# Attention block: the bias and the sums of weights in other slots

## The chip, the cores and the metric

One core of a Trainium2 chip runs the whole kernel. The metric is device time in microseconds, the median of several executions.

## The reference

One pre-norm layer of attention over 4096 tokens of width 1024, with 16 query heads and 4 key heads of 64, a causal window of 128, a learned bias per distance bucket and head, a sink per head, a SiLU gate, the residual, and a final norm:

```python
xn = rms_norm(x, norm_g)
q, k, v, z = split(xn @ w_in)                      # 1024, 256, 256, 1024 columns
s = q @ k.T / 8 + t5_table[bucket(distance)]       # distance 0 to 127 only
p = softmax([s, sink])[..., :-1]
y = ((p @ v) * silu(z)) @ w_out
out = rms_norm(x + y, final_g)
```

## The kernel before, in words

The tokens are cut into 16 blocks of 256. Each block has its projections q, k, v and z, four softmax pairs (a pair is 128 tokens and two key heads; each has two halves with steps scores, post, exps, normalise, turn, and then values and gate), and the output projection o. Every product in 16 bits is made of three passes over a high and a low half; the halves come from a split: ScalarE (ACT) writes the high half, VectorE (DVE) the low half.

A large product of two by two blocks can be done plainly with 8 block products, or as a chain of 7 with sums of blocks as factors (s1 to s4 on the weights, t1 to t4 on x for q and z; for o the sums s are of y and t of the weights). The first blocks run plainly, `PLAIN = {"q": 2, "z": 3, "o": 3}`, since the sums of weights must first be made. `sums` does that for four quarters c of each weight: it loads 1 MB of raw weights `wst`, scales it by the norm's gain (ACT), forms four sums on GpSimd (POOL, in place) and splits each. The q sums go to resident tiles `wq`, those of z and o to DRAM (`wzs`, `wos`; names such as `wzss1` are the tile of sum s1), from which four rotating buffers `ws` stream them. `wst` here has the tag of `xin`, the tile into which the next block's x rows are loaded for the norm, so both take turns in one buffer. `xf` is x transposed, `xb` and `xs` are the splits of it and of its sums.

The order of work is written as a table of slots: block tb starts at slot 25 tb, `at(phase, slot, f)` puts a piece of work there, and `emit` walks through slots and phases. Up to slot `STATIC` a scheduler then reorders each engine's instructions; behind it PE, ACT, DVE and POOL keep the written order. SyncE (SP) issues nearly all loads from one queue, ACT's queue issues the writes of split weights to DRAM.

`make_bias` forms a row of 256 biases per head on TensorE, writes 64 copies per head to DRAM (`scr`), and reads them back skewed by one element per copy, so that partition p holds the bias of query p. It is emitted at slot 8. `open_attn` closes the pool `ramp` of the first raw weights and opens the pool of the softmax tiles.

Of the kernel before, what the change touches and what calls it, by code (L numbers as in the profile page):

```python
# [58 lines left out]
def tile_swa_block(ctx, tc, x, xt, t5, norm_g, final_g, w_q, w_kv, w_z, sinks, w_out, hot, out):  # L59
# [68 lines left out]
    wq = [const.tile([P, 4, 2, 512], F16, name=f"wq{n}") for n in range(NRES)]  # L128
    wkv = const.tile([P, KC, 2, 512], F16, name="wkv")
    wqs = {n: dram.tile([P, 4, 2, 512], F16, name=f"wqs{n}") for n in range(NRES, 7)}  # L130
    wzs = {n: dram.tile([P, 4, 2, 512], F16, name=f"wzs{n}") for n in set(LEFT) | set(BLOCKS)}
    wos = {n: dram.tile([P, 4, 2, 512], F16, name=f"wos{n}") for n in set(RIGHT) | set(BLOCKS)}

    def split(hi, lo, f, scale):
        nc.scalar.activation(hi, f, AF.Copy, scale=scale)
        nc.vector.scalar_tensor_tensor(lo, f, scale, hi, op0=OP.mult, op1=OP.subtract)  # L136

    def load_kv(kc):
        st = work.tile([P, 512], F32, tag=("q00", "q01", "q10", "q11", "z00", "z01", "z10", "z11")[kc], name="wst",
                       bufs=1)  # L140
        nc.sync.dma_start(st, w_kv[kc * P:(kc + 1) * P, :])
        return st

# [6 lines left out]
    def factor(name, left, st):  # L150

        def blk(i, j):
            return st[:, j - 1, (i - 1) * 512:i * 512] if left else st[:, i - 1, (j - 1) * 512:j * 512]

        if name[0] not in "st":
            return blk(int(name[0]), int(name[1]))
        dst, l, r, op = {"s1": ((2, 1), (2, 1), (2, 2), OP.add), "s2": ((2, 1), (2, 1), (1, 1), OP.subtract),
                         "s3": ((1, 1), (2, 2), (2, 1), OP.subtract), "s4": ((1, 2), (1, 2), (2, 1), OP.subtract),
                         "t1": ((1, 2), (1, 2), (1, 1), OP.subtract), "t2": ((1, 2), (2, 2), (1, 2), OP.subtract),
                         "t3": ((1, 1), (1, 2), (1, 1), OP.subtract), "t4": ((2, 1), (2, 1), (1, 2), OP.subtract)}[name]  # L160
        nc.gpsimd.tensor_tensor(blk(*dst), blk(*l), blk(*r), op=op)  # L161
        return blk(*dst)
# [26 lines left out]

    def sums(w, c, left, to):  # L190

        st = work.tile([P, 2, D], F32, tag="xin", name="wst", bufs=1)
        load_pair(w, c, st)
        if left:
            for j in range(2):
                nc.scalar.activation(st[:, j, :], st[:, j, :], AF.Copy, scale=gs[:, 4 * j + c:4 * j + c + 1])  # L196
# [4 lines left out]
    def sum_q(n, name, c, f):  # L201
        if n < NRES:
            split(wq[n][:, c, 0], wq[n][:, c, 1], f, 1.0)
        else:
            to_dram(wqs[n], c, f, 1.0)

    def sum_z(n, name, c, f):
        to_dram(wzs[name], c, f, 1.0)

    def sum_o(n, name, c, f):  # L210
        to_dram(wos[name], c, f, SO)


    ji = const.tile([P, P], I32, name="ji")
    nc.gpsimd.iota(ji, pattern=[[1, P]], base=0, channel_multiplier=-1)
# [3 lines left out]
    nc.vector.tensor_scalar(own_m, ji, 0.0, None, op0=OP.is_ge)  # L219
    ij = const.tile([P, HD], I32, name="ij")  # L220
    for a in range(2):
# [3 lines left out]

    pre = const.tile([P, 2, P], F32, name="pre")
    nc.vector.memset(pre[:, 0, HD:], -BIG)
# [83 lines left out]
    def left_q(name):  # L311
        n = LEFT.index(name)
        return (lambda kc, wi: wq[n][:, kc, wi, :]) if n < NRES else stream("q", name)

# [141 lines left out]
    def make_bias():  # L456
        th = const.tile([BUCKETS, H], F32, name="th")
        nc.sync.dma_start(th, t5)
        hb = work.tile([BUCKETS, 2 * WIN], F32, tag="mc", name="hb", bufs=4)
        nc.sync.dma_start(hb, hot)  # L460
        s1 = const.tile([P, H], F32, name="s1")
        nc.sync.dma_start(s1, bass.AP(tensor=sinks.tensor, offset=sinks.offset, ap=[[0, P], [1, H]]))
        pe = ps("tp", 2)
        nc.tensor.matmul(pe[:H, :2 * WIN], th, hb, start=True, stop=True)
# [4 lines left out]
        for e in range(2):  # L469

            src = bass.AP(tensor=scr.tensor, offset=scr.offset + e * HD * 2 * WIN + HD - 1,
                          ap=[[2 * WIN - 1, HD], [2 * HD * 2 * WIN, H // 2], [1, HD + P]])
            nc.sync.dma_start(bias[e * HD:(e + 1) * HD], src)
# [196 lines left out]
    def at(phase, s, f, *a):  # L670
        work_of[s][phase].append(lambda: f(*a))
# [110 lines left out]

    def block(tb):
# [102 lines left out]
    for c in range(4):  # L886
        st = (work.tile([P, 2, D], F32, tag="ws", name="wst", bufs=4) if c < 3 else
              ramp.tile([P, 2, D], F32, tag="raw3", name="wst", bufs=1))
        raw["q", c] = load_pair(w_q, c, st)
    for c in range(3):  # L890
        raw["z", c] = load_pair(w_z, c, ramp.tile([P, 2, D], F32, tag=f"raw{c}", name="wst", bufs=1))
    for i in range(2):
        x_split(0, i)()
        for kc in range(4 * i, 4 * i + 4):
            split(wkv[:, kc, 0], wkv[:, kc, 1], kv[kc], gs[:, kc:kc + 1])
    for name in BLOCKS:
        for c in range(4):
# [12 lines left out]

# [49 lines left out]
```

## Time and profile before

| | |
|---|---|
| median of three runs | 1416.72 us (1415.52 to 1419.03) |
| profiled execution | 1415.16 us, span 1413.4 us |
| busy: PE, DVE, ACT, POOL | 95%, 83%, 62%, 29% |
| mean granted TensorE clock | 0.989 |
| moved by DMA | 371.96 MB, 263 GB/s |

Line numbers (L327) are those of the kernel before. A name like `c<-s,bias` says what an instruction writes and reads. L327 are the products of q and z, L346 and L408 those of k and v, L506 the scores, L562 the transposes of the weights p, L589 the products with v, L631 the products of o, L464 the bias, L531 and L533 the bias add and the row maximum, L161 the sums on POOL, L135 and L136 the two halves of a split, L196 the scaling of raw weights.

### The profile page before, as it was taken

The numbers are of one execution on the slowest core, as the hardware profiler recorded it, in microseconds if no ns is written. First come the engines' busy times: TensorE is split into PE (matmuls) and PEld (weight loads), VectorE is DVE, ScalarE is ACT, GpSimd is POOL, SyncE is SP. The second block draws the span as 40 slices with busy tenths as digits, with TensorE's granted clock in tenths as the row PEclk, the third lists the DMA queues.
The fourth block names the chain that finished last, engine by engine and source line by source line (L and its number), as shares of the span: only waits on it lengthen the run. The fifth ranks groups of instructions, "written<-read, shape, count | busy, mean of one in ns | idle before, by whom it ended". The sixth has DMA issues, their size and how long they took to land.

```text
span 1413.4 us, 39463 instructions
## 1 busy us (share of the span) xinstructions
PE 1348.6 (95%) x16234; PEld 1086.1 (77%) x16234; DVE 1175.1 (83%) x2847; ACT 878.4 (62%) x2313; POOL 416.3 (29%) x402
## 2 busy tenths in 40 slices
PE   5888999898989999999999999999999999999986
PEld 4887668587578787978788797978879687888842
DVE  7579787778769889798988979898888989888884
ACT  7466666666556566566666656666566666666662
POOL 1001342434323233241322324142322424141124
PEclk9999999999999999999999999999999999999999
DMA  9985657878969677684948767594966769384665
GB/s 370 276 303 183 252 193 299 308 256 325 367 237 334 219 281 270 216 340 168 348 180 297 266 236 300 206 343 159 337 240 250 270 227 353 142 318 176 246 231 208
DMA packets 73253, 371.96 MB, mean 263 GB/s; under 512 B 9040, under 2 KB 11120, under 8 KB 41456
## 3 DMA queue, kind: packets, MB, share of 16 engines
q1 hardware_dynamic: 63968, 351.61, 68.3%
q10 hardware_dynamic: 9104, 17.83, 3.3%
q8 instruction: 127, 2.08, 0.6%
q14 instruction: 54, 0.44, 0.1%
HBM read 332.71 MB, written 36.70 MB: 261 GB/s over the span
## 4 chain that ended last, share of the span: by engine, by line
PE 72%; DVE 10%; DMA 8%; ACT 6%; issue 2%; POOL 2%; SPq 0%; POOLq 0%; ACTq 0%; DVEq 0%
PE pb L327 14%; PE pa L327 14%; PE pc L631 9%; PE o L589 5%; PE pa L631 5%; PE pc L327 5%; PE s L506 5%; PE pc L408 4%; PE pb L346 4%; PE tp L562 3%; PE pb L631 3%; DMA wzs<-ws 1%; DVE wsp L136 1%; DMA wst<-in_wz 1%; POOL wst L161 1%
## 5 line engine op out<-in xcount | busy, mean ns | idle before, releaser
L327 PEld LDWEIGHTS <-ws 128*128 128x128 f16 x6864 | 391.8, 98 | 30.3 <-issue 26.7
L631 PEld LDWEIGHTS <-yo 128*128 128x128 f16 x1380 | 134.0, 99 | 159.9 <-issue 9.3
L327 PEld LDWEIGHTS <-wq 128*128 128x128 f16 x4128 | 237.2, 98 | 15.7 <-issue 10.5
L541 ACT ACTIVATE c<-c,m 128x129 f32<-128x129 f32 x512 | 198.5, 391 | 24.6 <-DVE m L533 24.1
L631 PE MATMUL pc<-ws,yo 128*128 128x512 f16 x768 | 178.1, 382 | 5.1 <-DMA ws<-wos 2.4
L533 DVE CUSTOM_DVE_ANT_0 c<-s,bias,sink 128x128 f32<-128x128 f32 x496 | 153.4, 349 | 7.5 <-PE tp L562 0.3
L247 POOL TENSOR_TENSOR rr<-ms,mhalf 128x1 f32<-128x1 f32 x64 | 36.8, 582 | 353.1 <-DVE ms L245 288.7
L569 DVE SCALAR_TENSOR_TENSOR pt<-tp,pt 128x512 f16<-128x512 f32 x128 | 87.5, 685 | 49.1 <-ACT pt L566 48.9
L553 ACT ACTIVATE c<-c,rl 128x128 f32<-128x128 f32 x256 | 86.8, 393 | 62.7 <-DVE rl L546 62.0
L625 DVE TENSOR_TENSOR yo<-y,yo 128x512 f16<-128x512 f32 x103 | 85.1, 827 | 45.6 <-ACT yo L624 45.4
L506 PE MATMUL s<-K,q 128*128 128x192 f16 x1024 | 109.5, 246 | 12.1 <-DVE m L533 6.1
L549 DVE TENSOR_SCALAR c<-c,rl 128x128 f32<-128x128 f32 x256 | 116.5, 497 | 4.0
L356 ACT ACTIVATE mc<-pa 128x512 f32<-128x512 f32 x68 | 40.5, 595 | 120.0 <-PE pa L327 111.7
L327 PE MATMUL pb<-xb,ws 128*128 128x128 f16 x1776 | 108.5, 221 | 6.2 <-issue 3.9
L161 POOL TENSOR_TENSOR wst<-wst 128x512 f32<-128x512 f32 x48 | 69.9, 1467 | 145.1 <-ACT wst L196 84.4
L327 PE MATMUL pb<-xs,ws 128*128 128x128 f16 x1872 | 111.0, 219 | 0.0
L506 PEld LDWEIGHTS <-q 128*128 128x128 f16 x1024 | 85.3, 98 | 27.5 <-issue 8.2
L570 DVE TENSOR_TENSOR pm<-pt,own_m 128x1024 f16<-128x1024 f16 x128 | 97.5, 761 | 3.7
L617 POOL TENSOR_TENSOR y<-y,y 128x512 f32<-128x512 f32 x52 | 78.9, 1518 | 70.2 <-DVE y L596 48.6
L285 POOL TENSOR_TENSOR xf<-xf 128x512 f32<-128x512 f32 x56 | 74.8, 1347 | 83.4 <-DVE xb L274 74.4
L541 ACT ACTIVATION_READ_ACCUMULATOR c<-c,m 128x1 f32 x512 | 96.5, 188 | 0.0
L631 PE MATMUL pa<-ws,yo 128*128 128x512 f16 x384 | 92.7, 393 | 3.8 <-DVE z L449 3.1
(122 smaller groups left out, 2648.2 us busy)
## 6 DMA issues: line engine op xcount, KB each, us to landing
ws<-wos SPq DMA_DIRECT2D x63, 1024.0 KB, 6.4
ws<-wzss SPq DMA_DIRECT2D x52, 1024.0 KB, 6.6
ws<-wost SPq DMA_DIRECT2D x52, 1024.0 KB, 6.0
ws<-wzs SPq DMA_DIRECT2D x47, 1024.0 KB, 6.2
ws<-wqs SPq DMA_DIRECT2D x28, 1024.0 KB, 5.9
xin<-in_x SPq DMA_DIRECT2D x32, 512.0 KB, 4.6
xf<-in_xt SPq DMA_DIRECT2D x32, 512.0 KB, 4.3
r<-in_x SPq DMA_DIRECT2D x32, 512.0 KB, 5.7
```

The costliest lines, as they stand in the source:

```text
L161: nc.gpsimd.tensor_tensor(blk(*dst), blk(*l), blk(*r), op=op)
L327: nc.tensor.matmul(place(p, c), left(kc, wi)[:, c * P:(c + 1) * P], right_x(tb, right, kc, xi), start=fresh and c == 0 and k == 0, stop=c ...
L506: nc.tensor.matmul(s[:, hp, 0:3 * HD], lhs, rhs, start=hl == 0, stop=hl == 1)
L533: nc.vector.tensor_tensor_reduce(out=cu, in0=sv, in1=b, scale=-1.0 / SCORE, scalar=sink[:, g, r, hp:hp + 1], op0=OP.add, op1=OP.min, accum ...
L541: nc.scalar.activation(cu, cu, AF.Exp, bias=self.m[:, u:u + 1], scale=-1.0, accum_out=self.l[:, u:u + 1])
L549: nc.vector.tensor_scalar(cu[u], cu[u], rl[:, u:u + 1], None, op0=OP.mult)
L553: nc.scalar.activation(cu[u], cu[u], AF.Copy, scale=rl[:, u:u + 1])
L569: nc.vector.scalar_tensor_tensor(w[:, 1], p, SP, w[:, 0], op0=OP.mult, op1=OP.subtract)
L570: nc.vector.tensor_tensor(m.rearrange("p l (h q) -> p (l h) q", h=4), w.rearrange("p l (h q) -> p (l h) q", h=4), own_m[:, None, :].to_bro ...
L617: nc.gpsimd.tensor_tensor(Y[(tb, *dst)], Y[(tb, *l)], Y[(tb, *r)], op=op)
L625: return lambda: nc.vector.tensor_tensor(yo[:, 1], s, yo[:, 0], op=OP.subtract)
L631: nc.tensor.matmul(p, YO[left][:, yi, c * P:(c + 1) * P], right(c, wi), start=fresh and k == 0, stop=k == 11, skip_group_check=not fresh)
```

## The change

The bias is made first: its inputs are loaded right behind block 0's x, the copies are 16 per head in place of 64, and the skewed bias is read in 8 pieces of 16 partitions in place of 2 of 64, behind the raw q weights. The pairs of block 0 stand 4, 3, 2 and 1 slots earlier, and the softmax pool opens at slot 12 in place of 18. `sums` is taken apart into steps with slots of their own and takes a buffer of its own, `stage`. The quarters of q, z and o start at slots 15, 39 and 63, six slots apart (before: 38 to 50, 63 to 75, 88 to 100), and `STATIC` falls from 105 to 90. All q sums go through DRAM; s1 and s2 come back into the plain blocks' tiles `wq[1]` and `wq[2]`, and s3 is streamed for blocks 2 to 4 and then kept in `stage`. The sums are formed in an order that overwrites other blocks. In blocks 0 to 2 the splits of the next x stand later (`PLAIN_X`). Of the differences dv one buffer is left in place of two. At the start the splits of w_kv are written ahead of those of x.

```diff
+    load_xin(0)
+    th = const.tile([BUCKETS, H], F32, name="th")
+    nc.sync.dma_start(th, t5)
+    hb = work.tile([BUCKETS, 2 * WIN], F32, tag="mc", name="hb", bufs=4)
+    nc.sync.dma_start(hb, hot)
+    load_xf(0)
+    nc.scalar.dma_start(gs, norm_g.rearrange("(c p) -> p c", p=P))
+    s1 = const.tile([P, H], F32, name="s1")
+    nc.scalar.dma_start(s1, bass.AP(tensor=sinks.tensor, offset=sinks.offset, ap=[[0, P], [1, H]]))
...
-    NRES = 5
-    STATIC = 105
+    STATIC = 90
+    SUMS = {"q": 15, "z": 39, "o": 63}
+    FIFTH = 5
...
-        st = work.tile([P, 2, D], F32, tag="xin", name="wst", bufs=1)
-        load_pair(w, c, st)
+        keep = []
+        def load():
+            keep.append(load_pair(w, c, work.tile([P, 2, D], F32, tag="stage", name="wst", bufs=1)))
+        def scale(j):
+            nc.scalar.activation(keep[0][:, j, :], keep[0][:, j, :], AF.Copy, scale=gs[:, 4 * j + c:4 * j + c + 1])
+        at("load", s, load)
         if left:
             for j in range(2):
-                nc.scalar.activation(st[:, j, :], st[:, j, :], AF.Copy, scale=gs[:, 4 * j + c:4 * j + c + 1])
-        for n, name in enumerate(LEFT if left else RIGHT):
-            if name[0] in "st":
-                to(n, name, c, factor(name, left, st))
+                at("high", s + 3, scale, j)
+        for i, (n, name) in enumerate((n, name) for n, name in enumerate(LEFT if left else RIGHT) if name[0] in "st"):
+            at("sum", s + 4 + i // 2, lambda name=name: keep.append(factor(name, left, keep[0])))
+            at_split(s + 5 + i // 2, lambda n=n, name=name, i=i: to(s + 5 + i // 2, n, name, c, keep[1 + i]))
+    def sum_to(s, where, c, f, scale):
+        w = work.tile([P, 2, 512], F16, tag="wsp", name="wsp", bufs=3)
+        nc.scalar.activation(w[:, 0], f, AF.Copy, scale=scale)
+        at("turn", s + 1, lambda: nc.scalar.dma_start(where[:, c], w))
+        return lambda: nc.vector.scalar_tensor_tensor(w[:, 1], f, scale, w[:, 0], op0=OP.mult, op1=OP.subtract)
...
-        scr = dram.tile([H, HD, 2 * WIN], F32, name="scr")
-        nc.sync.dma_start(scr, row[:, None, :].to_broadcast([H, HD, 2 * WIN]))
+        COPIES = 16
+        scr = dram.tile([H, COPIES, 2 * WIN], F32, name="scr")
+        nc.sync.dma_start(scr, row[:, None, :].to_broadcast([H, COPIES, 2 * WIN]))
...
-                 zplain=(11, 12, 13, 14, 15, 16, 17, 17), xload=8, pairs=moved(STEADY["pairs"], (7, 5, 4, 2)))
+                 zplain=(11, 12, 13, 14, 15, 16, 17, 17), xload=8, pairs=moved(STEADY["pairs"], (3, 2, 2, 1)))
...
+    PLAIN_X = dict(xsplit=(21, 22), xsum={"t1": 22, "t2": 24, "t3": 26, "t4": 27},
+                   xsumsplit={"t1": 23, "t2": 25, "t3": 29, "t4": 28})
...
-            for n in range(NRES, 7):
+            for n in range(4 if tb < FIFTH else 5, 7):
                 at("load", S["q"][n] - 4, load_s, "q", LEFT[n], wqs[n])
...
-    at("load", 8, make_bias)
-    work_of[18]["bank"].insert(0, open_attn)
+    work_of[12]["bank"].insert(0, open_attn)
...
-        at("soft", SLOTS + (13, 17, 21, 25)[c], sums, w_q, c, True, sum_q)
+        sums(SUMS["q"] + 6 * c, w_q, c, True, sum_q)
...
+    for n in (1, 2):
+        at("load", SLOTS * PLAIN["q"] - 6 + n, lambda n=n: nc.sync.dma_start(wq[n], wqs[n]))
+    at("load", SLOTS * FIFTH - 10, load_fifth)
```

What the scheduler made of it, at three places. First SyncE's queue from the start. Before:

```order
L99 DMA xin<-in_x 128x1024 x2
L105 DMA xf<-in_xt 128x1024 x2
L141 DMA wst<-in_wkv 128x512 x8
L147 DMA wst<-in_wq 128x1024 x8
L147 DMA wst<-in_wz 128x1024 x6
L99 DMA xin<-in_x 128x1024 x2
L105 DMA xf<-in_xt 128x1024 x2
L458 DMA th<-in_t_table 32x16
```

And in the change (its line numbers differ: L111 is L141, L156 is L147, L488 the write of the copies, L496 the skewed read):

```order
L99 DMA xin<-in_x 128x1024 x2
L116 DMA th<-in_t_table 32x16
L118 DMA hb<-in_hot 32x256
L105 DMA xf<-in_xt 128x1024 x2
L497 DMA gf<-in_final_g 128x1024
L111 DMA wst<-in_wkv 128x512 x3
L488 DMA scr<-row 256x1x256
L111 DMA wst<-in_wkv 128x512 x5
L156 DMA wst<-in_wq 128x1024 x8
L496 DMA bias<-scr 16x8x192 x8
L156 DMA wst<-in_wz 128x1024 x6
```

The whole bias, with the final gain gf, now stands ahead of the raw z weights, and five of the eight loads of w_kv and all of w_q stand behind the write of the copies.

Second DVE, where block 0's first softmax steps stand. Before, behind the evacuations of z and the first splits of w_out (`wsp<-r`):

```order
L449 SCALAR_TENSOR_TENSOR z<-z,pb 128x512
L136 SCALAR_TENSOR_TENSOR wsp<-r,wsp 128x512 x2
L449 SCALAR_TENSOR_TENSOR z<-z,pc 128x512
...
L274 TENSOR_TENSOR xb<-xf,xb 128x4x256
L524 COPY_PREDICATED s<-sel,s 128x2x64 x2
L531 TENSOR_TENSOR c<-s,bias 128x128 x4
```

In the change, ahead of the first of them (L473 is L449, L548 is L524, L555 is L531; `wsp<-wst` is the first quarter of q's sums):

```order
L151 SCALAR_TENSOR_TENSOR ws<-wst,gs,ws 128x512 x2
L284 TENSOR_TENSOR xf<-xf,tp 128x1024 x2
L221 SCALAR_TENSOR_TENSOR wsp<-wst,wsp 128x512
...
L548 COPY_PREDICATED s<-sel,s 128x2x64
L151 SCALAR_TENSOR_TENSOR ws<-wst,gs,ws 128x512 x2
L221 SCALAR_TENSOR_TENSOR wsp<-wst,wsp 128x512 x2
L264 TENSOR_SCALAR ms<-rs 128x1
L555 TENSOR_TENSOR c<-s,bias 128x128 x2
```

The first bias add moved from behind block 1's split of x (`xb`) to among the last splits of the raw z weights.

Third SyncE's queue where block 3's x is loaded. Before, behind z's last quarter of raw weights:

```order
L147 DMA wst<-in_wz 128x1024 x2
L306 DMA ws<-wzs_94 128x4096
L306 DMA ws<-wzss_97 128x4096
L306 DMA ws<-wzss_90 128x4096
L99 DMA xin<-in_x 128x1024 x2
L660 DMA out<-r 128x1024 x2
L147 DMA wst<-in_wo 128x1024
```

In the change the x rows of blocks 2 and 3 stand ahead of block 1's first z weights:

```order
L156 DMA wst<-in_wq 128x1024 x2
L156 DMA wst<-in_wz 128x1024 x2
L935 DMA wqs_97<-wq_90 128x4096
L99 DMA xin<-in_x 128x1024 x2
L156 DMA r<-in_wo 128x1024 x2
L99 DMA xin<-in_x 128x1024 x2
L325 DMA ws<-wzs_100 128x4096
```

The loads of x stand apart from those of raw weights for the sums, up to two blocks ahead of their use.

More of the change, by code (lines that the diff above doesn't have):

```diff
@@ L124, in tile_swa_block @@
     BLOCKS = ("11", "12", "21", "22")
-    NRES = 5
-    STATIC = 105
+    STATIC = 90
+    SUMS = {"q": 15, "z": 39, "o": 63}
+    FIFTH = 5
     HOME = {"11": 0, "21": 1, "22": 2, "12": 3}
-    wq = [const.tile([P, 4, 2, 512], F16, name=f"wq{n}") for n in range(NRES)]
+    wq = [const.tile([P, 4, 2, 512], F16, name=f"wq{n}") for n in range(4)]
     wkv = const.tile([P, KC, 2, 512], F16, name="wkv")
-    wqs = {n: dram.tile([P, 4, 2, 512], F16, name=f"wqs{n}") for n in range(NRES, 7)}
+    wqs = {n: dram.tile([P, 4, 2, 512], F16, name=f"wqs{n}") for n in (1, 2, 4, 5, 6)}
     wzs = {n: dram.tile([P, 4, 2, 512], F16, name=f"wzs{n}") for n in set(LEFT) | set(BLOCKS)}
@@ L136, in split @@
         nc.vector.scalar_tensor_tensor(lo, f, scale, hi, op0=OP.mult, op1=OP.subtract)
[L138 to L142, printed above, removed]
     def load_pair(w, c, st):
@@ L188, in plain_o, with sums, sum_q, sum_z @@
             to_dram(wos[name], c, factor(name, False, st), SO)
-    def sums(w, c, left, to):
-        st = work.tile([P, 2, D], F32, tag="xin", name="wst", bufs=1)
-        load_pair(w, c, st)
+    def sums(s, w, c, left, to):
+        keep = []
[4 more added lines that the diff above has]
+        at("load", s, load)
         if left:
             for j in range(2):
-                nc.scalar.activation(st[:, j, :], st[:, j, :], AF.Copy, scale=gs[:, 4 * j + c:4 * j + c + 1])
-        for n, name in enumerate(LEFT if left else RIGHT):
-            if name[0] in "st":
-                to(n, name, c, factor(name, left, st))
[L201 to L214, printed above, removed]
+                at("high", s + 3, scale, j)
[7 more added lines that the diff above has]
+        return lambda: nc.vector.scalar_tensor_tensor(w[:, 1], f, scale, w[:, 0], op0=OP.mult, op1=OP.subtract)
+    def sum_q(s, n, name, c, f):
+        return sum_to(s, wqs[n], c, f, 1.0)
+    def sum_z(s, n, name, c, f):
+        return sum_to(s, wzs[name], c, f, 1.0)
+    def sum_o(s, n, name, c, f):
+        return sum_to(s, wos[name], c, f, SO)
+    ji = work.tile([P, 512], I32, tag="mc", name="ji", bufs=4)[:, :P]
     nc.gpsimd.iota(ji, pattern=[[1, P]], base=0, channel_multiplier=-1)
@@ L219, in tile_swa_block @@
     nc.vector.tensor_scalar(own_m, ji, 0.0, None, op0=OP.is_ge)
-    ij = const.tile([P, HD], I32, name="ij")
+    ij = work.tile([P, 512], I32, tag="mc", name="ij", bufs=4)[:, :HD]
     for a in range(2):
@@ L224, in tile_swa_block @@
     nc.vector.tensor_scalar(sel, ij, 0.0, None, op0=OP.is_ge)
-    pre = const.tile([P, 2, P], F32, name="pre")
+    pre = work.tile([P, 4, P], F32, tag="xt4", name="pre", bufs=1)
     nc.vector.memset(pre[:, 0, HD:], -BIG)
@@ L312, in left_q, with load_fifth @@
         n = LEFT.index(name)
-        return (lambda kc, wi: wq[n][:, kc, wi, :]) if n < NRES else stream("q", name)
+        return (lambda kc, wi: wq[n][:, kc, wi, :]) if n < len(wq) else stream("q", name)
+    def load_fifth():
+        w = work.tile([P, 4, 2, 512], F16, tag="stage", name="wq4", bufs=1)
+        nc.sync.dma_start(w, wqs[4])
+        wq.append(w)
     def left_q_plain(name):
@@ L438, in split_dv @@
         d = DF.pop(tb)
-        dv = work.tile([P, 2, 2, NKV], F16, tag="dv", name="dv", bufs=2)
+        dv = work.tile([P, 2, 2, NKV], F16, tag="dv", name="dv", bufs=1)
         DV[tb] = dv
@@ L466, in make_bias, with spread @@
         nc.vector.tensor_scalar(row, pe[:H, :2 * WIN], SCORE, None, op0=OP.mult)
-        scr = dram.tile([H, HD, 2 * WIN], F32, name="scr")
-        nc.sync.dma_start(scr, row[:, None, :].to_broadcast([H, HD, 2 * WIN]))
[L469 to L473, printed above, removed]
+        COPIES = 16
+        scr = dram.tile([H, COPIES, 2 * WIN], F32, name="scr")
+        nc.sync.dma_start(scr, row[:, None, :].to_broadcast([H, COPIES, 2 * WIN]))
+        def spread():
+            for e in range(2):
+                for i in range(0, HD, COPIES):
+                    src = bass.AP(tensor=scr.tensor, offset=scr.offset + e * COPIES * 2 * WIN + HD - 1 - i,
+                                  ap=[[2 * WIN - 1, COPIES], [2 * COPIES * 2 * WIN, H // 2], [1, HD + P]])
+                    nc.sync.dma_start(bias[e * HD + i:e * HD + i + COPIES], src)
         nc.sync.dma_start(gf, bass.AP(tensor=final_g.tensor, offset=final_g.offset, ap=[[0, P], [1, D]]))
@@ L479, in make_bias @@
                                         None, op0=OP.mult)
+        return spread
     class Pair:
@@ L790, in there @@
             return tuple(s0 + s for s in v) if isinstance(v, tuple) else s0 + v
+        isplain = {n: tb < m for n, m in PLAIN.items()}
+        if isplain["z"]:
+            plan = dict(plan, **PLAIN_X)
         S = {k: there(v) for k, v in plan.items()}
-        isplain = {n: tb < m for n, m in PLAIN.items()}
         if isplain["q"]:
```

27 lines of the change are left out of this document (14 added, 13 removed).

## Prediction

> **What bounds the kernel now.** I read the page first, then a table of six stretches of the span, then who waits for whom on TensorE in the stretches where it is not full, and last the chain of waits through the first 130 us.
>
> ```profile
> PE 1348.6 (95%) x16234; PEld 1086.1 (77%) x16234; DVE 1175.1 (83%) x2847; ACT 878.4 (62%) x2313; POOL 416.3 (29%) x402
> PE   5888999898989999999999999999999999999986
> ```
>
> TensorE is busy for 95% of the span, and the digits of its row show that the missing 5% is not spread out: slices of 8 and less stand at the start and at the end. The table by stretch says it in microseconds; its columns are the stretch, its length, the busy time of PE, PEld, DVE, ACT and POOL, the granted TensorE clock, the share of the 16 DMA engines, and GB/s.
>
> ```profile
> 0.00:50.00 50.00, 34.94 (x423) 30.71 (x424) 41.14 (x75) 40.28 (x65) 4.89 (x15) 0.97 0.94 351
> 50.00:90.00 40.00, 32.50 (x538) 32.08 (x536) 15.21 (x33) 13.27 (x25) 2.47 (x4) 0.96 0.98 297
> 90.00:200.00 110.00, 100.52 (x1162) 77.93 (x1160) 96.12 (x273) 75.01 (x208) 31.61 (x26) 0.97 0.59 212
> 200.00:430.00 230.00, 214.08 (x2547) 171.68 (x2545) 182.90 (x438) 141.78 (x351) 81.36 (x71) 0.99 0.80 293
> 430.00:1323.00 893.00, 893.00 (x10974) 730.19 (x10973) 777.52 (x1879) 563.06 (x1536) 268.10 (x262) 1.00 0.70 258
> 1323.00:1413.40 90.40, 73.61 (x606) 43.51 (x604) 62.26 (x156) 45.00 (x130) 27.86 (x26) 0.95 0.65 236
> ```
>
> From 430 to 1323 us TensorE is busy for 893.00 of 893.00 us at full clock. The change leaves the work on TensorE as it is, so those eleven blocks give nothing, and the tail (the last block's slots) is not edited. Whatever the change is worth lies before 430 us. There TensorE is idle for 15.1, 7.5, 9.5 and 15.9 us, and the clock takes a little more: (1 - 0.96) x 40 = 1.6, (1 - 0.97) x 110 = 3.3, (1 - 0.99) x 230 = 2.3. From 50 to 430 us that is 32.9 + 7.2 = 40.1 us, the pool from which the change can draw; the first 50 us are loads and splits of raw weights, which stay.
>
> The chain of waits says what held block 0 (start us, length, what):
>
> ```profile
> 45.95 0.55 PE tp L464 x2
> ...
> 48.41 20.41 DMA wzs<-ws
> 68.84 15.85 DMA bias<-scr
> ...
> 84.81 0.30 DVE c L531
> ```
>
> The bias's matmul runs at 46 us, yet the first softmax step starts at 84.8: the write of 64 copies per head, the z weights written behind it, and the read of the skewed bias lie between. DVE is busy only 15.2 of the 40 us from 50 to 90, and 96.1 of 110 just after. In the first twenty of those it is full:
>
> ```profile
> 90.00:100.00 10.00, 10.00 (x165) 9.99 (x163) 9.87 (x52) 8.51 (x33) 0.00 (x0) 1.00 0.89 353
> 100.00:110.00 10.00, 10.00 (x171) 9.96 (x170) 9.90 (x39) 8.25 (x25) 0.20 (x1) 1.00 0.41 142
> ```
>
> Two blocks' softmaxes and the splits of weights meet there.
>
> **The hole at 60 us.** First what TensorE waited for from 50 to 90 us and, in the fourth row, the second largest wait from 90 to 200 (in total, times, longest), then three stretches with the columns above.
>
> ```profile
> PE pb L327 <- issue: 3.9, 1, 3.9
> PE pb L327 <- ACT xb L272: 1.9, 1, 1.9
> PE s L506 <- DVE c L531: 1.7, 1, 1.7
> PE pa L631 <- DVE z L449: 3.1, 1, 3.1
> 48.00:60.00 12.00, 12.00 (x217) 11.99 (x215) 3.08 (x5) 1.48 (x3) 0.33 (x2) 1.00 0.83 95
> 65.60:69.00 3.40, 3.40 (x36) 3.40 (x33) 1.07 (x2) 0.00 (x0) 0.00 (x0) 0.50 1.03 426
> 178.30:185.00 6.70, 5.91 (x14) 2.09 (x15) 6.70 (x10) 2.09 (x4) 6.59 (x5) 0.50 0.56 183
> ```
>
> From 48 to 60 us the DMA engines are 83% busy and move 95 GB/s, against 351 over the first 50 us: this is the 1 MB of copies, in pieces of 1 KB. Right behind it TensorE stands still for 3.9 us with "issue", waiting for no data, and then runs 3.4 us at half clock, worth 1.7. I read the hole as TensorE's instructions arriving late behind the copies. With 16 copies the write is 0.25 MB, about 12 / 4 = 3 us, and is done near 10 us. I count 3.9 + 1.7 = 5.6 us gained; bounds 0 (the hole has another cause) and 5.6.
>
> The page "TensorE: Matmul & The Clock Gate" of the Trainium skill (Part 1: The HAM clock gate) says that the clock falls to half after a whole idle window of about 3.4 us. By that only the 3.9 us hole could cost clock. The trace differs: the stretch from 178.3 to 185.0 also runs at 0.50, behind the wait of 3.1 us. By the page the next term but one, 9, would be 3.3 us smaller and the sum 17.9; I go by the trace.
>
> **Block 0's softmax earlier.** The bias wait (1.7) goes. The 1.9 for xb of block 1 is the split of x, which must wait for block 0's last z product in either kernel; scores and transposes now stand in it, so I take half, 0.9. Gain 2.6, bounds 1.7 and 3.6. DVE takes from 90 us on into its free 24.8 us (40 - 15.2) before:
>
> ```profile
> L531 DVE TENSOR_TENSOR c<-s,bias 128x128 f32<-128x128 f32 x16 | 3.7, 285 | 3.0 <-DMA bias<-scr 2.9
> L533 DVE CUSTOM_DVE_ANT_0 c<-c,pre,sink 128x128 f32<-128x128 f32 x16 | 5.0, 346 | 0.0
> L570 DVE TENSOR_TENSOR pm<-pt,own_m 128x1024 f16<-128x1024 f16 x8 | 6.0, 748 | 0.0
> L569 DVE SCALAR_TENSOR_TENSOR pt<-tp,pt 128x512 f16<-128x512 f32 x8 | 5.4, 684 | 1.7 <-ACT pt L566 1.7
> PE s L506 <- DVE m L533: 3.2, 3, 1.7
> ```
>
> The 16 bias adds and the 16 steps that follow them move whole (8.7 us), and of the four p splits and masks of the first pairs about half of 11.4, so some 14 us leave a stretch in which every wait on TensorE ends with DVE or behind it (the last row here, the largest from 90 to 200 us, and the 3.1 us above). Its pool is 9.5 idle + 3.3 clock = 12.8. Bounds 3.2 (the softmax waits alone) and 12.8; I take 9, nearer the upper end, since the 3.1 us row drags the half clock with it.
>
> **Sums in slots of their own, with a buffer of their own.** Before, the sums' raw weights share one buffer with x.
>
> ```profile
> by line: DMA wzs<-ws 5.1%; DVE wsp L136 4.4%; DMA wst<-in_wz 4.4%; issue 4.2%; DMA bias<-scr 4.0%; ACT wst L196 3.9%; ACT c L541 3.8%; PE pb L327 3.6%; POOL wst L161 3.2%; DMA xin<-in_x 3.2%; DVE c L533 2.9%; DMA wos<-wsp 2.8%; PE pa L327 2
> 289.55 6.73 DMA wst<-in_wz
> ...
> 312.22 7.21 DMA xin<-in_x
> PE pb L631 <- DMA ws<-wos: 2.8, 1, 2.8
> PE pc L631 <- DMA ws<-wos: 2.4, 1, 2.4
> ```
>
> Up to 400 us the chain (first row) runs through wst, its scaling and sums, and through xin: block 3's x is loaded at 312 us behind z's last raw weights at 290. Freed of that, x comes up to two blocks ahead in SyncE's order. TensorE's waits from 200 to 430 (the last two rows are the two on streamed weights; the others are 0.2 to 2.5) sum to its 15.9 idle, plus 2.3 of clock. Those two are loads queued on SyncE behind raw weights; the new order still puts raw weights among them, so they need not go. I take 8 of 18.2, under half; bounds 0 and 15.
>
> **What it costs.** The sums of q go through DRAM now:
>
> ```profile
> ws<-wqs SPq DMA_DIRECT2D x28, 1024.0 KB, 5.9
> s<-in_a_sinks SPq DMA_DIRECT2D x1, 8.0 KB, 8.6
> ...
> 53.41 5.52 PE L327 MATMUL pa<-xb,ws 128*128 128x128 f16 x96
> 186.40 0.68 DVE L292 TENSOR_TENSOR xs<-xf,xs 128x512 f16<-128x512 f32 x1
> 195.24 2.84 PE L327 MATMUL pa<-xb,wq 128*128 128x128 f16 x48
> ```
>
> 12 more pieces of 256 KB are written, and 6 more MB read (two into resident tiles, one for each of blocks 2 to 4, one at the end): 9 MB. At 293 GB/s this is 31 us of transfers; free are 0.41 x 110 + 0.20 x 230 = 91 us from 90 to 430, which hide them unless one load comes late. ACT issues the 12 writes behind its splits, SyncE the six reads. The second resident load stands on SyncE behind block 3's x, which waits for block 2's third sum of x. In the trace that sum's split ends at 187.1 us and TensorE begins the q chain at 195.2 (last two rows), 8 us of lead, and a load lands in 5.9 (first row), so I price one late load at a third: 2 us, bounds 0 and 6. One more streamed load per block is covered by the four weight buffers. In the first 50 us gf (0.5 MB) and the copies (0.25 MB) go ahead of most of w_kv: 0.75 MB / 351 GB/s = 2.1 us; and DVE now has the sink's four steps ahead of x's second factor, waiting for a load that took 8.6 us: 0 to 4 us. DVE and ACT, 41 and 40 of 50 us busy, hide part of it; I take 2 in all, bounds 0 and 5. The eight bias reads in place of two move the same bytes; z's last weights were written out from 48.4 us on, 5 us before TensorE took them at 53.4 (third row), and these 5 us cover the reads.
>
> Sum: 5.6 + 2.6 + 9 + 8 - 2 - 2 = 21.2 us off the profiled execution's 1415.2 (span 1413.4 and 1.8 around it): 1394.0. The median of the three runs is 1.5 above it, so 1395.5. All gains at their upper ends and no cost: 5.6 + 3.6 + 12.8 + 15 = 37.0, 1379.7. All gains but the hole low, the costs as taken: 5.6 + 1.7 + 3.2 + 0 - 4 = 6.5, 1410.
>
> **Rivals.**
> Hidden anyway: the splits of q's and z's sums move into the room that the softmax leaves, so DVE is as full from 90 to 200 us and what goes after 200 comes back. Then 5.6 + 2.6 - 4 = 4.2 remain: 1412.5. For it: the sums' splits, DVE wsp with 4.4% in the chain's row above, all stay. Against it: DVE at 777.5 of 893 us, 87%, holds up nothing in the full blocks.
> All of it: 1380, if the first four blocks run like the rest. Against it: SyncE's one queue still mixes raw weights with streamed ones.
> The hole stays, if the copies did not cause it: 1395.5 + 5.6 = 1401.1. For it: nothing in the page joins "issue" to a queue. Against it: it ends as the copies do.
> The half clock at 178 us was not the doing of the 3.1 us wait: 3.3 less is gained, 1398.8. For it speaks the page on the clock gate. Against it: the two rows above.
> Slower: SyncE's order. In blocks 2 to 4 each q chain now needs a load more, and the two resident ones wait behind x. A load issued when TensorE already wants it costs 5.9 us, on average half of x's 7.2 (the row of xin) in front of it, and the half clock 1.7: 11.2 in a block, 33.6 in three, in place of the 2 priced: 1427. From 9.2 us a block (27.5 in all) it is slower by over 0.3%. The eight microseconds of lead speak against it.
>
> **How the numbers follow.** 0.3% is 4.25 us, about what a measurement of this kernel tells from no change. Forecast 0.45; all of it 0.12; the hole stays 0.1; the clock 0.05; hidden anyway 0.18, half of it over 0.3% and half within; slower 0.1. So faster 0.45 + 0.12 + 0.1 + 0.05 + 0.09 = 0.81, same 0.09, slower 0.1. The range runs from the full gain to the rival of a hidden one: 1379 to 1413.
>
> **What would show it.** Right: no "issue" wait near 60 us and no stretch of 12 us near 95 GB/s after 20 us; the first c<-s,bias step before 65 us; DVE over 20 of 40 us from 50 to 90; x rows of block 3 before 330 us; and TensorE idle under 20 us from 50 to 430. Wrong: waits of TensorE on wq or ws<-wqs over 3 us, a first product later than 15 us, or DVE over 97% from 80 to 180 us.

## The result, and the profile after

The changed kernel takes 1395.89 us (median of five runs, 1395.08 to 1396.57) against 1417.92 for the kernel before on the same chip: a ratio of 0.9847, 95% interval 0.9833 to 0.9862, some 22 us faster. Its profiled execution took 1396.40 us (span 1394.6), 18.8 below the 1415.16 of before. The first four stretches of the changed kernel and the full blocks behind them, with the columns of the table by stretch shown of before:

```profile
0.00:50.00 50.00, 32.70 (x367) 28.29 (x368) 38.66 (x68) 36.91 (x58) 3.64 (x11) 0.93 0.90 314
50.00:90.00 40.00, 36.87 (x584) 35.69 (x582) 26.87 (x73) 25.86 (x56) 9.29 (x11) 0.92 1.02 416
90.00:200.00 110.00, 103.66 (x1263) 83.23 (x1262) 97.30 (x267) 79.70 (x213) 29.56 (x27) 1.00 0.75 278
200.00:430.00 230.00, 223.18 (x2736) 181.33 (x2734) 191.28 (x446) 139.45 (x354) 84.96 (x72) 0.99 0.85 318
430.00:1304.00 874.00, 874.00 (x10693) 713.52 (x10691) 761.49 (x1842) 551.52 (x1505) 261.45 (x255) 1.00 0.71 256
```

TensorE's idle time (length less the first number) goes from 15.1, 7.5, 9.5 and 15.9 us to 17.3, 3.1, 6.3 and 6.8. The full blocks are as they were, a full TensorE at full clock. By these rows, from 50 to 430 us the pool of 40.1 falls to 16.3 idle and 5.5 of clock, 18.3 less; the first 50 us lose 2.2 idle and 2.0 of clock more. That makes 14.1 of the 18.8 us. Where the rest lies these rows do not show; a clock of two digits alone leaves some of it open (0.005 of 230 us is 1.2 us).

What TensorE waits for now (lines are those of the changed kernel: L351 is L327 of before, L370 L346, L482 L464, L530 L506, L555 L531, L557 L533, L586 L562, L655 L631), the largest rows up to 50 us, all rows from 50 to 90, the largest from 90 to 200, and the largest from 200 to 430 (in total, times, longest):

```profile
PE tp L482 <- DMA hb<-in_hot: 8.8, 1, 8.8
PE pa L370 <- ACT wkv L150: 4.1, 1, 4.1
PE pb L351 <- ACT v L447: 2.6, 1, 2.6
PE tp L586 <- DVE c L573: 0.9, 1, 0.9
PE pb L351 <- DVE xb L293: 0.9, 1, 0.9
PE pb L351 <- ACT xb L291: 0.6, 1, 0.6
PE tp L586 <- ACT c L577: 0.6, 1, 0.6
PE s L530 <- DVE m L557: 3.2, 2, 1.7
PE pc L655 <- DMA ws<-wos: 3.2, 1, 3.2
```

No "issue" wait is left near 60 us, no wait on `ws<-wqs`, none on `wq` after the first 50 us (the longest there is 0.7), and the wait of 3.1 us behind DVE near 178 us is gone. The first bias add comes at 65.9 us (before: 84.8):

```profile
L555 DVE TENSOR_TENSOR c<-s,bias x16: 281/282/286, 65.9 to 94.5; 128x128 f32<-128x128 f32 x16
```

And SyncE's queue, where x is loaded: first the loads of blocks 3 and 4 before, then the same two blocks' loads in the change (start us, us, what).

```profile
202.46 0.81 SPq L99 DMA_DIRECT2D xin<-in_x  x2
312.22 0.90 SPq L99 DMA_DIRECT2D xin<-in_x  x2
```

```profile
65.66 4.39 SPq L99 DMA_DIRECT2D xin<-in_x  x2
91.16 2.49 SPq L99 DMA_DIRECT2D xin<-in_x  x2
```

Counted from the start, the load at 312 us is that of block 4. The prediction and the words ahead of the third piece of order call it block 3's, which is a slip of one block. With its own buffer x now comes more than 200 us earlier, and TensorE takes the row of norm factors that is made from it (`rr`) 12 us earlier (320.5 us, before 332.4).

### The profile page after: what moved, and what is told of

Same layout as the page of the kernel before. It is cut to its first block, busy times and chain, and to the rows that moved or that the text cites. A ratio compares the mean times of both kernels' runs of the same rounds, so it can differ in the third digit from the quotient of the medians.

```text
span 1394.6 us, 39512 instructions
## 1 busy us (share of the span) xinstructions
PE 1344.0 (96%) x16234; PEld 1085.8 (78%) x16234; DVE 1178.0 (84%) x2847; ACT 878.5 (63%) x2313; POOL 416.8 (30%) x402
## 4 chain that ended last, share of the span: by engine, by line
PE 75%; DVE 10%; DMA 8%; issue 2%; ACT 2%; POOL 1%; SPq 1%; ACTq 0%; POOLq 0%; DVEq 0%
PE pa L351 15%; PE pb L351 15%; PE pc L655 9%; PE pb L370 6%; PE o L613 6%; PE pc L432 5%; PE s L530 5%; PE pc L351 5%; PE pa L655 5%; PE tp L586 3%; PE pb L655 2%; DMA wst<-in_wz 2%; DVE c L557 2%; DMA wst<-in_wq 2%; DVE wsp L221 1%
## 5 line engine op out<-in xcount | busy, mean ns | idle before, releaser
L351 PEld LDWEIGHTS <-ws 128*128 128x128 f16 x7008 | 397.1, 98 | 20.1 <-issue 16.3
L655 PEld LDWEIGHTS <-yo 128*128 128x128 f16 x1380 | 133.4, 98 | 154.9 <-issue 11.0
L351 PEld LDWEIGHTS <-wq 128*128 128x128 f16 x3984 | 232.4, 99 | 16.5 <-issue 10.5
L655 PE MATMUL pc<-ws,yo 128*128 128x512 f16 x768 | 177.9, 382 | 7.4 <-DMA ws<-wos 4.6
L557 DVE CUSTOM_DVE_ANT_0 c<-s,bias,sink 128x128 f32<-128x128 f32 x496 | 153.6, 349 | 7.5 <-PE tp L586 0.3
L573 DVE TENSOR_SCALAR c<-c,rl 128x128 f32<-128x128 f32 x256 | 113.4, 484 | 3.9
L530 PE MATMUL s<-K,q 128*128 128x192 f16 x1024 | 107.9, 246 | 5.6 <-DVE m L557 5.2
L351 PE MATMUL pb<-xs,ws 128*128 128x128 f16 x1872 | 111.0, 219 | 0.0
L351 PE MATMUL pb<-xb,ws 128*128 128x128 f16 x1776 | 106.8, 219 | 0.0
L530 PEld LDWEIGHTS <-q 128*128 128x128 f16 x1024 | 85.6, 98 | 19.3 <-DVE m L557 7.5
L590 ACT ACTIVATE pt<-tp 128x512 f16<-128x512 f32 x128 | 74.2, 593 | 40.1 <-PE tp L586 29.8
L380 ACT ACTIVATE mc<-pb 128x512 f32<-128x512 f32 x53 | 31.6, 597 | 107.4 <-PE pb L351 71.8
```

Source lines behind the costliest of these rows:

```text
L351: nc.tensor.matmul(place(p, c), left(kc, wi)[:, c * P:(c + 1) * P], right_x(tb, right, kc, xi), start=fresh and c == 0 and k == 0, stop=c ...
L530: nc.tensor.matmul(s[:, hp, 0:3 * HD], lhs, rhs, start=hl == 0, stop=hl == 1)
L557: nc.vector.tensor_tensor_reduce(out=cu, in0=sv, in1=b, scale=-1.0 / SCORE, scalar=sink[:, g, r, hp:hp + 1], op0=OP.add, op1=OP.min, accum ...
L573: nc.vector.tensor_scalar(cu[u], cu[u], rl[:, u:u + 1], None, op0=OP.mult)
L655: nc.tensor.matmul(p, YO[left][:, yi, c * P:(c + 1) * P], right(c, wi), start=fresh and k == 0, stop=k == 11, skip_group_check=not fresh)
```

## Experiments

Ratios are against the kernel before, run with each series; the interval is 95%. The changed kernel itself stands at 0.9847 (0.9833 to 0.9862).

| kernel | median us | ratio (interval) |
|---|---|---|
| before, 16 copies | 1404.45 | 0.9894 (0.9878 to 0.9910) |
| the same, 1 MB more in small pieces | 1422.39 | 1.0034 (1.0018 to 1.0049) |
| the same, 1 MB more in large pieces | 1412.12 | 0.9959 (0.9945 to 0.9973) |
| before, 16 copies and a buffer for the sums | 1413.03 | 0.9971 (0.9956 to 0.9987) |
| change, block 0's pairs at old slots | 1395.49 | 0.9831 (0.9812 to 0.9851) |
| change, bias at slot 8 | 1397.15 | 0.9860 (0.9840 to 0.9880) |
| change, cheaper start | 1397.65 | 0.9862 (0.9845 to 0.9878) |
| change, sums in the buffer of x | 1417.22 | 0.9984 (0.9971 to 0.9997) |
| change, sums of z and o later | 1399.54 | 0.9863 (0.9845 to 0.9882) |
| change, steps of the sums in one burst | 1396.19 | 0.9855 (0.9834 to 0.9876) |
| change, writes of the sums at once | 1395.79 | 0.9855 (0.9839 to 0.9872) |
| change, STATIC 105 | 1399.09 | 0.9870 (0.9855 to 0.9885) |

**Fewer copies alone.** In the kernel before:

```diff
-        scr = dram.tile([H, HD, 2 * WIN], F32, name="scr")
+        COPIES = 16
+        scr = dram.tile([H, COPIES, 2 * WIN], F32, name="scr")
...
+            for i in range(0, HD, COPIES):
```

> The kernel before with one edit: 16 copies of the bias per head in place of 64, read back in 8 pieces, at the old place (slot 8). Theory 1 (the copies made the hole at 60 us): the issue wait of 3.9 us and the half clock behind it (1.7) go, the write between 48 and 60 us takes about 3 us in place of 12, and the wait of the first scores on the bias (1.7) goes too: 5.6 to 7.3 us less than before, about 1411 (1408 to 1413). Theory 2 (the hole has another cause): an issue wait near 60 us stays, and the time is 1416 to 1419.

It gave more than either theory: 1404.45, a ratio of 0.9894, some 15 us; its profiled execution took 1404.71, 10.5 less than before's. By stretch, 50 to 90, 90 to 200 and 200 to 430 us:

```profile
50.00:90.00 40.00, 39.88 (x685) 39.55 (x683) 23.83 (x76) 21.24 (x51) 2.35 (x3) 1.00 0.95 355
90.00:200.00 110.00, 100.23 (x1139) 76.61 (x1137) 98.83 (x266) 77.81 (x214) 34.93 (x31) 0.97 0.64 227
200.00:430.00 230.00, 216.44 (x2597) 175.13 (x2595) 181.62 (x418) 138.09 (x336) 78.82 (x69) 0.97 0.79 290
```

TensorE is full from 50 to 90 us: not the hole alone but all 7.5 us of idle time there and the clock's 1.6 are gone, so the waits on the bias and on xb go with it. Behind 90 us little is changed: 9.8 and 13.6 us idle, where before had 9.5 and 15.9, but from 200 us on the clock is 0.97 in place of 0.99, worth 4.6 us the other way. By these rows the kernel gains 6.4 us (9.0 - 0.3 + 2.3 - 4.6); what made the rest of its 10.5 they do not show.

**Which bytes make the hole.** Two kernels add 1 MB behind the 16 copies, to a DRAM tile that nobody reads:

```diff
+        spare = dram.tile([H, HD, 2 * WIN], F32, name="spare")
+        nc.sync.dma_start(spare, row[:, None, :].to_broadcast([H, HD, 2 * WIN]))
```

```diff
+    spare = dram.tile([P, 4, 2, 512], F16, name="spare")
+    at("load", 8, lambda: nc.sync.dma_start(spare, WS["z", "12"]))
```

> The kernel with 16 copies (1404.45) and one write more, behind the copies: 1 MB from the row of the bias to a DRAM tile that nobody reads, 64 copies per head in pieces of 1 KB out of 16 partitions, as the old copies were. Theory 1 (the small pieces hold back TensorE's instructions): an issue wait of 3 to 4 us comes back near 60 us, with a half clock behind it. Theory 2 (what stood there was a wait that the profile does not name, for the bias or z weights): no issue wait; the bias read behind it makes the first scores wait, by name. Time 1409 to 1413 by 1, 1405 to 1411 by 2.

> The kernel with 16 copies (1404.45) and the same 1 MB written at the same place in SyncE's queue, but out of 128 partitions in large pieces (a z tile copied to a DRAM tile that nobody reads). Theory 1 (the small pieces are the cause, not the bytes): no issue wait, the write takes about 3 to 6 us; 1403 to 1406. Theory 2 (any 1 MB in that place does it): an issue wait of over 2 us near 60 us and 1408 or more.

With the small pieces, TensorE's longest wait from 50 to 90 us, and the write's row among the DMA issues (KB, us from issue to landing):

```profile
PE pc L327 <- issue: 3.5, 1, 3.5
```

```profile
spare<-row SPq DMA_DIRECT2D x1, 1024.0 KB, 26.8
```

With the large ones, the same 40 us, and the write's row:

```profile
50.00:90.00 40.00, 40.00 (x693) 39.96 (x691) 24.97 (x78) 20.70 (x53) 2.45 (x5) 1.00 0.98 366
```

```profile
spare<-ws SPq DMA_DIRECT2D x1, 1024.0 KB, 11.1
```

The small pieces bring the hole back, the same bytes in large pieces do not, and the eight reads of the bias are the same in both. So the write of the copies made the hole, and nothing waited for their data. The two writes differ in more than their pieces, though: the small ones come out of 16 partitions, the large ones out of 128, and these were not tried apart. How the write holds TensorE, the instruction queue shows: between 48 and 61.5 us no block started in the kernel before, and with 16 copies

```profile
q8 instruction: 1, 0.02, 0.4%
```

one block of 16 KB. In the kernel with the small pieces none starts from 60 to 70 us, and TensorE stands from 69.1 to 72.7. The page "Runtime: NRT & Kernel Launch" of the Trainium skill (Instruction fetch mechanics) says that an engine fetches its instructions in blocks of 16 KiB through a DMA queue and that this is mostly hidden; here it was not. That it is TensorE's own block that is late, the counts say. This queue over the whole span, and the work up to the hole in the kernel before and in the one with the small pieces (the two numbers with an x that come first are matmuls and weight loads):

```profile
q8 instruction: 127, 2.08, 0.6%
0.00:62.00 62.00, 45.44 (x606) 41.07 (x607) 42.41 (x77) 42.54 (x69) 5.54 (x16) 0.97 0.93 309
0.00:70.30 70.30, 53.63 (x734) 49.20 (x735) 47.56 (x84) 44.96 (x73) 6.33 (x17) 0.95 0.93 321
```

The 127 blocks share out the span's 16234 matmuls and as many weight loads at 256 a block. TensorE stops after 1213 of them in the one kernel and after 1469 in the other: just one block later. While it stands, a block does come (between 62 and 63 us, and from 70.35 us on), and it goes on at 64.4 and 72.7. What keeps that block behind the write, no row shows.

The times of both kernels lie above their bands: 1422.39, where theory 1 had 1409 to 1413, and 1412.12, where it had 1403 to 1406; the large write took 11.1 us, where 3 to 6 were expected.

The times have a second lesson. The large pieces cost nothing where they stand, and yet the kernel is 0.65% slower than the one with 16 copies alone (0.9959 against 0.9894). TensorE loses it later: it is idle for 21.2 us from 200 to 430, with 16 copies alone for 13.6. The scheduler orders the first four blocks anew around any edit; the two orders of DVE already differ from the splits just ahead of block 0's softmax on. I take it that this is where the 9 us come from, which was not tried by itself, and read no difference of that size in this table as an edit's own without a row that shows how.

**Block 0's softmax at its old slots.**

```diff
-                 zplain=(...), xload=8, pairs=moved(STEADY["pairs"], (3, 2, 2, 1)))
+                 zplain=(...), xload=8, pairs=moved(STEADY["pairs"], (7, 5, 4, 2)))
```

> The changed kernel with block 0's softmax pairs back at their old slots, 7, 5, 4 and 2 behind the steady ones in place of 3, 2, 2 and 1. Theory 1 (the earlier softmax relieves DVE from 90 us on; the terms of 2.6 and 9): TensorE's idle time from 50 to 200 us rises from 9.4 by 5 or more, time 1402 to 1408. Theory 2 (the scheduler starts the softmax when the bias is there, whatever its slot, or the relief comes from elsewhere): 1395 to 1399.

1395.49: theory 2. Set back alone, the slots of block 0's softmax are worth nothing that the times show (its trace, of its slowest execution with 1401.13 us, has 11.9 us idle from 50 to 200, the changed kernel 9.5).

**The bias at slot 8.**

```diff
-    spread_bias = make_bias()
+    at("load", 8, lambda: make_bias()())
```

with the loads of `th`, `hb`, `s1` and `gf` inside, as before.

> The changed kernel with the bias back at slot 8, its small loads and the final gain with it; 16 copies. Theory 1 (the bias first is only a cost: the queue stands for it at 9 to 14 us and at 22 to 34 us, and an earlier softmax is worth nothing, as with the old pair slots): first product at 12 us, one half-clock window less before 50 us, time 1390 to 1393. Theory 2 (without the early bias block 0's first scores wait and the softmaxes of two blocks meet again): idle 50 to 200 us above 12 us, time 1398 to 1403.

1397.15, between the two bands and nearer to theory 2, whose sign came: 13.4 us idle from 50 to 200. The start is as quick as before, and the next stretch loses it. All four stretches (of its slowest execution, 1400.12):

```profile
0.00:50.00 50.00, 34.50 (x428) 30.36 (x429) 39.08 (x71) 40.28 (x64) 5.04 (x14) 0.97 0.96 369
50.00:90.00 40.00, 32.19 (x530) 31.77 (x528) 22.19 (x39) 15.04 (x27) 8.25 (x8) 0.91 0.94 325
90.00:200.00 110.00, 104.38 (x1259) 83.66 (x1258) 103.19 (x301) 84.36 (x237) 32.30 (x30) 1.00 0.77 288
200.00:430.00 230.00, 221.90 (x2735) 180.68 (x2736) 191.69 (x442) 139.76 (x355) 83.79 (x71) 1.00 0.84 317
```

From 90 to 200 us DVE is busy for 103.2 of 110 us, more than in any other kernel here, and TensorE is idle for 5.6, less than in the changed kernel. So a fuller DVE alone does not hold TensorE up there.

**A cheaper start.**

```diff
-        nc.sync.dma_start(gf, ...)
+    at("load", 30, lambda: nc.sync.dma_start(gf, ...))
...
-        nc.sync.dma_start(scr, row[:, None, :].to_broadcast([H, COPIES, 2 * WIN]))
+        nc.scalar.dma_start(scr, row[:, None, :].to_broadcast([H, COPIES, 2 * WIN]))
...
-    spread_bias()
     for c in range(3):
         raw["z", c] = load_pair(w_z, c, ...)
+    spread_bias()
```

> The changed kernel with a cheaper start: the final gain is loaded at slot 30 in place of ahead of w_kv, the copies are written from ACT's queue so that SyncE does not stand for them, and the eight bias reads stand behind the raw z weights. The bias still comes early. Theory 1 (SyncE standing still at 9 to 14 us and at 22 to 34 us is what the start lost, 2.7 us of first product and one half-clock window of 1.7): first product at about 12 us, TensorE idle near 15 us before 50 us, time about 1391.5 (1390 to 1393). Theory 2 (the start is bounded by the splits on DVE and ACT, or what is won there is lost at the next wait): 1395 to 1397.

The step that theory 1 names came true and the time did not. The first product comes at 12.95 us (in the changed kernel at 14.6) and TensorE's idle time up to 50 us is 14.8; but the next stretch loses it again:

```profile
0.00:50.00 50.00, 35.17 (x428) 30.29 (x429) 38.63 (x70) 36.76 (x59) 5.02 (x13) 0.97 0.91 321
50.00:90.00 40.00, 33.47 (x523) 31.70 (x521) 26.62 (x68) 25.09 (x54) 8.31 (x9) 0.96 1.01 400
```

and TensorE's largest wait from 50 to 90 us:

```profile
PE pa L351 <- DVE ws L151: 2.1, 2, 1.4
```

That is 6.5 us idle in place of 3.1, the largest wait now on the splits of the raw z weights. By 90 us both kernels have run 951 matmuls (428 + 523 here, 367 + 584 in the changed kernel). 1397.65 lies just above theory 2's band. What the bias costs at the start, the z weights would have cost 40 us later.

**The sums in the buffer of x.**

```diff
-            keep.append(load_pair(w, c, work.tile([P, 2, D], F32, tag="stage", name="wst", bufs=1)))
+            keep.append(load_pair(w, c, work.tile([P, 2, D], F32, tag="xin", name="wst", bufs=1)))
```

> The changed kernel with the sums' raw weights back in the buffer of x (stage is then used for the fifth tile alone); slots as changed. Theory 1 (the buffer of their own lets x come early, the term of 8 us): x rows of block 3 come after 325 us, TensorE's idle time from 200 to 430 us rises from 6.8 to 13 or more, and the time is about 1404 (1400 to 1410). Theory 2 (the slots six apart do it, the buffer does not): 1395 to 1398, with x rows as in the changed kernel.

1417.22, nearly all of the gain gone. From 200 to 430 us, the stretch and TensorE's longest wait:

```profile
200.00:430.00 230.00, 204.55 (x2401) 163.84 (x2399) 172.38 (x408) 130.69 (x327) 73.70 (x63) 0.94 0.77 284
```

```profile
PE tp L279 <- POOL rr L266: 14.3, 3, 8.3
```

25.5 us idle, 14.3 of them on the row of norm factors, since x comes late as theory 1 says (block 4's at 346 us, in the changed kernel at 91), and 0.06 x 230 = 13.8 us of clock. The time lies above theory 1's band: the price is more than twice the 8 us expected.

**The buffer without the rest.** The kernel before with 16 copies and

```diff
-    NRES = 5
+    NRES = 4
...
-        st = work.tile([P, 2, D], F32, tag="xin", name="wst", bufs=1)
+        st = work.tile([P, 2, D], F32, tag="stage", name="wst", bufs=1)
```

> The kernel before with two edits: 16 copies in place of 64 at the old place, and a buffer of their own for the sums' raw weights (paid for by one resident tile of q less, so the sum s3 is streamed in every block). The sums keep their old slots in bursts. With 16 copies alone the time was 1404.45. Theory 1 (the buffer is the second part of the gain, whatever the slots): 1395 to 1399, x rows of block 3 before 320 us. Theory 2 (the buffer pays only with the sums spread over slots of their own): 1402 to 1406. Theory 3 (as 2, and the load more in every block costs): above 1406.

1413.03, above 1406: theory 3's band, though not by its reason, since the load more costs nothing in the full blocks. x comes early here too (block 4's at 89 us), and yet TensorE is idle for 20.7 us from 200 to 430, the longest wait that of the scores:

```profile
200.00:430.00 230.00, 209.27 (x2446) 166.76 (x2446) 179.37 (x409) 129.86 (x316) 78.28 (x66) 0.96 0.81 296
```

```profile
PE s L506 <- DVE m L533: 8.6, 3, 6.3
```

They wait for the row maximum, behind splits of late sums on DVE and ACT. The buffer alone is not enough.

**What else it takes.** Four kernels take one more piece of the change back.

```diff
-                at("high", s + 3, scale, j)
...
-            at("sum", s + 4 + i // 2, ...)
-            at_split(s + 5 + i // 2, ...)
+        at("soft", s + 4, burst)
```

> The changed kernel with the steps of a quarter of sums in one burst again, as before: scaling, four sums, four splits and their writes all at slot s + 4, where the change spreads them over s + 3 to s + 7. The buffer of their own and the quarters six slots apart stay. Theory 1 (spreading the steps is what lets the buffer pay: in a burst DVE's splits and ACT's writes stand ahead of the softmax): TensorE idle from 90 to 430 us rises from 13.1 to 22 or more, time 1404 to 1413. Theory 2 (the earlier start of the quarters does it, or the rest of the change): 1395 to 1400.

```diff
-        at("turn", s + 1, lambda: nc.scalar.dma_start(where[:, c], w))
...
+            nc.scalar.dma_start(where[:, c], w)
```

> The changed kernel with one edit: ACT issues the write of a split right behind DVE's low half, in the same slot, as before, and not a slot later. Theory 1 (ACT stands behind DVE for these writes, and the exponentials behind ACT): 1399 to 1406, with waits of ACT on DVE's wsp. Theory 2 (ACT has room for it; in the scheduled part the order is chosen anyway): 1395 to 1398.

```diff
-    SUMS = {"q": 15, "z": 39, "o": 63}
+    SUMS = {"q": 15, "z": 51, "o": 76}
```

> The changed kernel with the sums of z and of w_out 12 and 13 slots later (51 and 76 in place of 39 and 63), in the buffer of their own. Theory 1 (the buffer is what matters, the place of the sums is not): 1395 to 1399. Theory 2 (the sums' early place matters, since they then run beside fewer softmax and output steps, or reach TensorE late as streamed weights): TensorE idle 12 us or more from 200 to 430 us, time 1401 to 1408.

```diff
-    STATIC = 90
+    STATIC = 105
```

> The changed kernel with STATIC back at 105: the scheduler orders 15 slots more, as before. Theory 1 (the written order or the scheduler's is the same to TensorE in these slots): 1394 to 1398. Theory 2 (the written order is part of the gain from 200 to 430 us): 1399 to 1405, with more waits of the scores on the row maximum there.

The burst (1396.19) and the writes at once (1395.79) change nothing: theory 2 in both. The later sums (1399.54) fall between their bands, the longer reach of the scheduler (1399.09) just inside theory 2's, though without its waits of the scores (1.4 us from 200 to 430, in the changed kernel 1.6). Both intervals overlap that of the change, and TensorE's idle time from 200 to 430 us is 8.3 and 9.7 us, under theory 2's 12 for the first. At most some 4 us hang on either, no more than the order may make. So what lets the buffer pay is neither the steps' spreading nor their writes. What is left is above all that the sums stand some 20 slots earlier (q's first at slot 19 in place of 38, z's at 43 in place of 63, o's at 67 in place of 88), further than the 12 and 13 by which the later sums were set back, and that the splits of x stand later in blocks 0 to 2 (`PLAIN_X`). Neither was tried by itself, nor were the smaller edits (the softmax pool's slot, the way of q's sums through DRAM, the single buffer of dv, the order of the first splits); which of them it is stays open.

## Why the prediction was right, and where not

The time came out: 1395.5 predicted, 1395.9 measured. That it did so this closely is luck. The profiled execution was forecast at 1394.0 and took 1396.4; the median was to lie 1.5 above it and lies 0.5 below. By stretch, idle time and clock together, the change gains 2.8 us from 50 to 90 (the hole and the softmax, 5.6 + 2.6, were to give 8.2), 6.4 from 90 to 200 (9) and 9.1 from 200 to 430 (8), and it loses 4.2 before 50 (2) and nothing for late loads (2). These rows make 14.1 us where the sum had 21.2, and up to 90 us nothing is won. What the forecast had right is where the time can come from, and that it comes.

- **The hole, 5.6.** The cause was read rightly, and the runs with small and large pieces show it. The term was mis-sized: with fewer copies alone it is 9.0 us by the rows from 50 to 90 us (7.4 idle, 1.6 clock), in a kernel that is 10 to 15 faster. I had counted the hole and its half clock; what stood behind the same queue, the bias and with it the 1.7 and 1.9 us of waits, belonged to it. In the changed kernel, with less idle time there too, a new half clock (0.92 from 50 to 90) takes 3.2 us where the old one took 1.6.
- **Block 0's softmax earlier, 2.6.** The waits are smaller, but the edit that I priced does nothing that shows: with the old slots, or the old place of the bias, the time is the same within the intervals. Fewer copies alone had already taken these waits away. The two were not set back together.
- **90 to 200 us, 9.** The trace gives 3.1 idle + 3.3 clock = 6.4, within the bounds. The step "some 14 us leave a stretch in which every wait on TensorE ends with DVE" failed: DVE is busy for 97.3 us there after and 96.1 before, and the kernel with the bias at slot 8 has DVE fuller and TensorE less idle.
- **The sums, 8.** Idle time falls by 9.1 us, the clock stays. That the buffer is needed was right (0.9984 without it, some 19 us); that "freed of that" x alone would do it was not, as the buffer without the rest shows.
- **Late loads, 2.** The 9 MB cost nothing that can be seen: no wait of TensorE on them.
- **The start, 2.** 4.2 us in the trace (2.2 idle, 2.0 clock), inside the bounds 0 to 5. The reason was in part another: SyncE stands for the row of the bias, and then at the reads, while w_kv and the raw z weights queue behind. How much of the loss is this and how much the final gain ahead of w_kv, which I had priced, stays open, since each run that moves the one moves the other. SyncE's largest wait up to 60 us, and three of its rows with start and length:

```profile
SPq L496 <- DMA wst<-in_wq: 11.1, 8, 2.6
```

```profile
10.31 0.67 SPq L488 DMA_DIRECT2D scr<-row  x1
11.02 4.38 SPq L111 DMA_DIRECT2D wst<-in_wkv  x5
21.48 12.42 SPq L496 DMA_DIRECT2D bias<-scr  x8
```

And as the cheaper start shows, this loss is one that the next stretch would take anyway.

Of the rivals, the clock one did not come: with the 3.1 us wait gone, the half clock near 178 us is gone (1.00 from 90 to 200). Hidden anyway did not come either, but something like it does where the sums keep their old places: the two kernels with 16 copies and the sums in their old slots are idle for 23.3 and 28.8 us from 90 to 430, before 25.4. Of the signs, the first bias add missed its mark by 0.9 us (65.9 against 65), and the first product its own by little on the good side (14.6 against 15); the others came as written.

## What to carry to other kernels

A write that repeats a short row many times, here in pieces of 1 KB out of 16 partitions, may cost far more than its bytes and stop an engine that waits for none of its data: look for "issue" next to a DMA share that is high at few GB/s. A term is priced by making that edit alone and by undoing it alone; of two edits that draw on the same wait, each may look worth it when made alone and worth nothing when undone alone. Where a scheduler orders the work, any edit reorders it, so a difference of half a per cent between single edits proves little without a look at the stretch it is meant to change.

## What the runs showed of the hardware that I had not expected

TensorE's clock falls without one long wait. In the changed kernel the longest single wait from 50 to 90 us is 0.9 us, but they crowd:

```profile
80.20:83.60 3.40, 1.84 (x13) 1.07 (x12) 1.78 (x8) 1.89 (x6) 0.00 (x0) 1.00 1.05 419
83.70:90.40 6.70, 5.24 (x49) 5.08 (x49) 6.15 (x17) 6.39 (x13) 0.20 (x1) 0.50 1.02 423
```

In 3.4 us TensorE is busy for 1.84, just over half, and the next 6.7 us run at half clock. The page "TensorE: Matmul & The Clock Gate" of the Trainium skill (Part 1: The HAM clock gate) speaks of a window of about 3.4 us that must be idle. The half-clock stretches here fit that length once or twice (3.4 and 6.7 us), but the stretch ahead of this one was not idle. Nor does a low busy share decide alone. In the kernel before, two stretches of the same length with less work stand between 80 and 90 us, and the clock stays full in them and behind (1.00 from 90 to 100 us):

```profile
82.70:86.10 3.40, 1.68 (x27) 1.51 (x25) 1.29 (x7) 0.96 (x1) 0.00 (x0) 1.00 1.01 364
86.10:89.50 3.40, 1.51 (x27) 1.39 (x25) 2.07 (x8) 3.40 (x9) 1.27 (x1) 1.00 1.01 420
```

So a stretch that is busy for half can be enough to lose the clock, and need not be. What tells the two apart was not tried.
